# A two-layer streaming encoder on one core: the ConvFFN down projection as seven block products instead of a plain product

## The chip, the core and the metric

One core of a Trainium2 chip runs the whole program, and the metric is the time of one execution on the device in microseconds. Of three timed executions of the kernel before the median is 1671.96 us (1671.85 to 1672.4). The engines are named as in the profile: PE multiplies matrices, PEld loads its stationary operand, DVE, ACT and POOL work on vectors (POOL also issues DMAs here after the change), and SP issues most DMAs.

## The reference

Two layers run over 512 prompt positions and 32 sample positions, with 1024 features. Each layer has a mixing block, cross-attention, and a convolutional feed-forward block of width 2816, the part that is changed:

```
g, up = jnp.split(h @ w_up, 2, axis=-1)
gp = jnp.concatenate([hist, g], axis=1)
c = conv_b + sum(conv_w[j] * gp[:, j:j + S] for j in range(CONV_W))
a = jax.nn.silu(c) * up
return a @ w_down, gp[:, -(CONV_W - 1):]
```

The result of `a @ w_down` is added to the residual `x`. Everything is float32.

## The kernel before

Activations lie feature-major: `x` is a tile of 128 partitions by 8 feature blocks by 544 positions (512 prompt and 32 sample), and a product's output for one feature block is two PSUM banks of 272 positions each (`NSPL`). Accuracy of float32 comes from splitting each operand into a high part that PE can take (fp32r) and the rest: ACT makes the high part, DVE subtracts it to get the low part, and PE multiplies high by high, high by low and low by high. So each block of 128 by 128 weights costs three matmuls per bank (`proj_fm`, L256 to L266).

Weights come through `emit_unit` (L124): SP loads a unit of up to 1024 float32 per partition into `raw` (three buffers), ACT casts it (L134), and DVE takes the rest (L135), both into one of four `hl` buffers. `pop` hands out two units and emits two more, so that the splitting runs one step ahead of PE. SP's next load of `raw` waits until DVE has finished with the buffer.

`do_ffn` (L898 to L962) works in two halves of 11 feature blocks each. For two blocks at a time PE makes the gate, DVE scales it and convolves, ACT takes a tanh, and then PE makes the up branch, DVE scales it and multiplies it in, and the product is split into an `at` tile (L174, L175). After a half's 11 blocks follows its share of the down projection: for each of 8 output blocks `ct`, 11 blocks of weights by three by two banks are 66 matmuls into `pfda` and `pfdb` (L958), and then two adds on DVE from PSUM into `x` (`update_x`, L210). After the second half `after(ct)` makes the next layer's operand (`set_h`: ACT L190, DVE L191, ACT L197, POOL L202), or, in the last layer, transposes `x` on PE and stores it (`final_x`, L964).

The framework simulates the program when it is built and sets the order of instructions on every engine from that; on the chip each engine then runs its own list in order. Semaphores make it wait for other engines and for DMAs.

Of the kernel before, what the change touches and what calls it, by code (L numbers as in the profile page):

```python
# [18 lines left out]
SP = 512  # L19
# [4 lines left out]
HF = NF // 2  # L24
# [10 lines left out]
def encoder_step(ctx: ExitStack, tc: tile.TileContext, a, o):  # L35
# [46 lines left out]
    units = []  # L82

    def build_units():
        for l in range(DEPTH):
            wi = a["w_in"][l]
            def ks(src, k0, n):
                return src[k0 * 128:(k0 + n) * 128].rearrange("(k p) c -> p k c", p=128)

            def two(tag, mat, cols):  # L90
                for k0 in (0, 4):
                    units.append((tag, [ks(mat[:, c:c + n], k0, 4) for c, n in cols], 4, sum(n for _, n in cols)))

# [6 lines left out]
            for j in range(4):  # L100
                src = a["w_out"][l][:, 256 * j:256 * j + 256].rearrange("(b q k p) c -> q b p k c", b=2, q=2, p=128)
                for q in range(2):
                    units.append((f"wout{j}", [src[q, 0], src[q, 1]], 4, 256))
# [6 lines left out]
            for hf in range(2):  # L110
                for f in range(hf * HF, hf * HF + HF, 2):
                    w = 128 * min(2, hf * HF + HF - f)
                    for nm, c0 in (("g", 0), ("up", FF)):
                        two(f"{nm}{f}", a["w_up"][l], [(c0 + 128 * f, w)])
                for ct in range(8):
                    for k0, n in ((0, 8), (8, HF - 8)):
                        units.append((f"dn{hf}_{ct}", [ks(a["w_down"][l][:, 128 * ct:128 * ct + 128],
                                                          hf * HF + k0, n)], n, 128))
# [3 lines left out]
    state = {"emitted": 0, "popped": 0}  # L122

    def emit_unit(i):  # L124
        tag, srcs, n, wc = units[i]
        raw = wp.tile([128, 1024], F32, tag="raw", bufs=3, name="raw")
        rv = raw[:, 0:n * wc].rearrange("p (k c) -> p k c", k=n)
        k0 = c0 = 0
        for v in srcs:
            kn, cn = v.shape[1], v.shape[2]  # L130
            sp.dma_start(out=rv[:, k0:k0 + kn, c0:c0 + cn], in_=v)
            k0, c0 = (k0, c0 + cn) if kn == n else (k0 + kn, c0)
        hl = wp.tile([128, 2, 1024], F32R, tag="hl", bufs=4, name="hl")
        act.copy(hl[:, 0, 0:n * wc], raw[:, 0:n * wc])  # L134
# [998 lines left out]
```

## Time and profile before

| | us |
|---|---|
| median of 3 | 1671.96 |
| the profiled execution | 1672.13 |
| its span, first to last instruction | 1670.4 |
| PE busy | 1647.6 |
| DVE busy | 1006.9 |
| ACT busy | 725.4 |
| POOL busy | 267.1 |

The profile comes from one execution. What it doesn't cover of that execution's time is 1672.13 - 1670.4 = 1.73 us. A row of a timeline has a start, a duration, an engine, a line of the code, the operation and its tiles, and in brackets the idle time before it with what ended it. Matmuls are pipelined, so that the distance between two starts, not a row's duration, is what one costs.

### The profile page before, as it was taken

To read this page: it belongs to the slowest core of one execution; us is meant where nothing else is said; L and a number is where in the kernel's file an instruction comes from. 1 tells how busy PE (TensorE), PEld (TensorE's weight loads), DVE (VectorE), ACT (ScalarE), POOL (GpSimd) and SP (SyncE) were. 2 spreads that over 40 slices of the span, in tenths; PEclk is the share of its full clock that TensorE was granted. 3 is DMA by queue.
4 is the path that set the end of the run, shared out by engine and by line. 5 is a ranking of instruction groups with operands and counts; after the bars stand their busy time and mean duration, and the time that the engine had idled before them with its cause. 6 is when DMAs were issued, how large, how long until landed. Compare 5 with 4: busy or idle time off the path is not lost.

```text
span 1670.4 us, 32582 instructions
## 1 busy us (share of the span) xinstructions
PE 1647.6 (99%) x13115; PEld 1619.0 (97%) x13115; DVE 1006.9 (60%) x2219; ACT 725.4 (43%) x1481; POOL 267.1 (16%) x718
## 2 busy tenths in 40 slices
PE   7999999999999999999999999999999999999998
PEld 6999999999999999999999999999999999999998
DVE  6779755655476625665358786655555664366642
ACT  5467654544333312333345685545443332233321
POOL 4110033222111000100121000432311110011100
PEclk9999999999999999999999999999999999999999
DMA  6323234332222233313332322244322222332231
GB/s 178 93 88 100 71 102 128 125 110 89 89 90 70 84 88 102 101 58 90 96 120 72 94 71 77 90 132 133 115 82 88 79 77 88 103 92 86 67 111 56
DMA packets 200989, 158.04 MB, mean 95 GB/s; under 512 B 8670, under 2 KB 200038, under 8 KB 200838
## 3 DMA queue, kind: packets, MB, share of 16 engines
q1 hardware_dynamic: 200774, 155.82, 30.6%
q8 instruction: 103, 1.69, 0.4%
q14 instruction: 48, 0.39, 0.1%
q10 hardware_dynamic: 64, 0.14, 0.0%
HBM read 144.83 MB, written 11.10 MB: 93 GB/s over the span
## 4 chain that ended last, share of the span: by engine, by line
PE 94%; DVE 2%; ACT 2%; issue 1%; POOL 1%; DMA 0%; ACTq 0%
PE pfda L262 8%; PE pfua L262 8%; PE pfga L262 8%; PE pfdb L262 8%; PE pfub L262 8%; PE pfgb L262 8%; PE pr L279 3%; PE pr L281 3%; PE pr L280 3%; PE pwob L262 3%; PE pwoa L262 3%; PE pwca L262 3%; PE pqb L262 3%; PE pqa L262 3%; PE pwcb L262 3%; PE pm L281 2%
## 5 line engine op out<-in xcount | busy, mean ns | idle before, releaser
L135 DVE TENSOR_TENSOR hl<-raw,hl 128x1024 fp32r<-128x1024 f32 (+2 forms) x280 | 315.3, 1127 | 253.9 <-ACT hl L134 253.5
L134 ACT CAST hl<-raw 128x1024 fp32r<-128x1024 f32 (+2 forms) x280 | 270.1, 965 | 399.2 <-PE pfdb L262 137.3
L262 PE MATMUL pfda<-at,hl 128*128 128x272 f32 x1056 | 266.6, 289 | 0.0
L262 PE MATMUL pfdb<-at,hl 128*128 128x272 f32 x1056 | 266.3, 288 | 0.0
L262 PE MATMUL pfga<-hx,hl 128*128 128x272 f32 x1056 | 263.8, 287 | 0.0
L262 PE MATMUL pfgb<-hx,hl 128*128 128x272 f32 x1056 | 263.7, 287 | 0.0
L262 PE MATMUL pfua<-hx,hl 128*128 128x272 f32 x1056 | 259.3, 287 | 0.8 <-ACT rbc L252 0.8
L262 PE MATMUL pfub<-hx,hl 128*128 128x272 f32 x1056 | 259.1, 287 | 0.0
L262 PEld LDWEIGHTS pfda<-at,hl 128*128 128x128 f32 x1056 | 199.2, 189 | 0.0
L262 PEld LDWEIGHTS pfdb<-at,hl 128*128 128x128 f32 x1056 | 198.7, 188 | 0.1
L262 PEld LDWEIGHTS pfga<-hx,hl 128*128 128x128 f32 x1056 | 198.6, 188 | 0.0
L262 PEld LDWEIGHTS pfgb<-hx,hl 128*128 128x128 f32 x1056 | 198.4, 188 | 0.0
L262 PEld LDWEIGHTS pfua<-hx,hl 128*128 128x128 f32 x1056 | 196.3, 188 | 1.1 <-ACT rbc L252 1.1
L262 PEld LDWEIGHTS pfub<-hx,hl 128*128 128x128 f32 x1056 | 196.2, 188 | 0.0
L280 PE MATMUL pr<-hl,hx 128*128 128x256 f32 x512 | 146.2, 286 | 1.8 <-DVE hl L135 1.8
L281 PE MATMUL pr<-hl,hx 128*128 128x256 f32 x512 | 146.4, 287 | 1.4 <-DVE hx L191 1.4
L279 PE MATMUL pr<-hl,hx 128*128 128x256 f32 x512 | 145.1, 284 | 2.2 <-DVE vs L305 0.9
L279 PEld LDWEIGHTS pr<-hl,hx 128*128 128x128 f32 x512 | 97.9, 192 | 3.8 <-DVE vs L305 1.4
L280 PEld LDWEIGHTS pr<-hl,hx 128*128 128x128 f32 x512 | 97.1, 190 | 2.3 <-DVE hl L135 2.0
L281 PEld LDWEIGHTS pr<-hl,hx 128*128 128x128 f32 x512 | 96.9, 190 | 2.2 <-DVE hx L191 1.8
L262 PE MATMUL pwcb<-co,hl 128*128 128x272 f32 x384 | 87.0, 288 | 0.0
L262 PE MATMUL pwca<-co,hl 128*128 128x272 f32 x384 | 87.0, 289 | 0.0
(365 smaller groups left out, 3345.1 us busy)
## 6 DMA issues: line engine op xcount, KB each, us to landing
raw<-in_w_up_dram SPq DMA_DIRECT2D x80, 512.0 KB
raw<-in_w_down_dram SPq DMA_DIRECT2D x32, 512.0 KB
raw<-in_w_in_dram SPq DMA_DIRECT2D x24, 512.0 KB
raw<-in_w_in_dram SPq DMA_DIRECT2D x32, 256.0 KB
raw<-in_w_out_dram SPq DMA_DIRECT2D x32, 256.0 KB
raw<-in_wq_c_dram SPq DMA_DIRECT2D x16, 512.0 KB
raw<-in_wk_c_dram SPq DMA_DIRECT2D x16, 512.0 KB
raw<-in_wv_c_dram SPq DMA_DIRECT2D x16, 512.0 KB
```

Of the source, the lines that this page charges most:

```text
L134: act.copy(hl[:, 0, 0:n * wc], raw[:, 0:n * wc])
L135: vec.tensor_tensor(out=hl[:, 1, 0:n * wc], in0=raw[:, 0:n * wc], in1=f32(hl[:, 0, 0:n * wc]), op=ALU.subtract)
L262: pe.matmul(out=ps[0 if n0 == 0 else 1][:, 0:nn], lhsT=hl[:, wpart, kk, col * 128:col * 128 + 128], rhs=mv[:, n0:n0 + nn], start=first and ...
L279: pe.matmul(out=out, lhsT=lh(k), rhs=hl[:, 0, k % 4], start=(k == 0), stop=False)
L280: pe.matmul(out=out, lhsT=lh(k), rhs=hl[:, 1, k % 4], start=False, stop=False)
L281: pe.matmul(out=out, lhsT=ll(k), rhs=hl[:, 0, k % 4], start=False, stop=(k == k8 - 1))
```

## The change

The contraction blocks are taken in pairs, the output blocks `ct` in pairs, and the two banks of positions are the other pair, so that the down projection is a product of 2 by 2 blocks, and seven block products (Strassen's, in Winograd's form) take the place of eight. The weights' sums S1 to S4 are made by POOL from two `raw` tiles, the activations' sums T1 to T4 by POOL from the unsplit `up` tiles; all are split into high and low parts as before.

The 11 pairs of blocks go in three parts of 3, 4 and 4 pairs. A part has four groups `j` (two output blocks each) of seven products, with n = 3 or 4 pairs contracted by each, so 3n matmuls of 272 columns. Each group has three banks. Bank `p7a` is summed in four steps: after A11·B11, after S2·T2 and after S3·T3 the running sum is copied out by ACT (`snap`) and added to a quarter of `x` by a DMA that accumulates, issued by POOL; after A22·T4 DVE adds it to `x`. The partial sums in the other two banks are added by DVE as well: `p7c` after S1·T1 and after S4·B22, and `p7b` after A12·B21. The seventh product of a group (A22) stands after the second product of the next group. The first pair of the next part is computed before a part's down projection.

`hl` now has eight half-sized buffers: a down product takes one, other units two. `raw` has three as before; a group needs two of them at once. The tanh's factor 0.5 goes into the convolution's weights, and POOL multiplies the gate by the row scale that DVE multiplied into the up branch.

```
-HF = NF // 2
+PARTS = ((0, 3), (3, 7), (7, 11))
...
+    raws, items = [], []
+    LAST = "A22"
+    ORDER = ("A11", "S1", "S2", "S4", "A12", "S3")
...
+                n = p1 - p0
+                before = None
+                for j in range(4):
+                    src = a["w_down"][l][256 * p0:256 * p1, 256 * j:256 * j + 256].rearrange(
+                        "(k e p) c -> e p k c", e=2, p=128)
+                    for e in range(2):
+                        raws.append([[(0, n, 0, 256, src[e])], n, None])
+                    ids = (len(raws) - 2, len(raws) - 1)
+                    for m, it in enumerate(ORDER):
+                        item(f"dn{q}_{j}", it, ids, n)
+                        if m == 1 and before is not None:
+                            item(f"dn{q}_{j - 1}", LAST, before, n)
+                    before = ids
+                item(f"dn{q}_3", LAST, before, n)
...
+    SLOTS, RAWS = 8, 3
...
+            (A11, A21), (A12, A22) = [[raw_t[r][:, :, 128 * c:128 * c + 128] for c in range(2)] for r in ids]
+            def summed(name, in0, in1, op):
+                t = tmp([128, 4, 128], name, tag="c2", bufs=3)[:, 0:n]
+                pool.tensor_tensor(out=t, in0=in0, in1=in1, op=op)
+                sums[name] = t
+            if what == "A11":
+                summed("S1", A21, A22, ALU.add)
+                summed("S2", sums["S1"], A11, ALU.subtract)
+            src = {"A11": A11, "A12": A12, "A22": A22}.get(what)
+            if src is None:
+                src = sums[what]
+            hl = wp.tile([128, 2, 4, 128], F32R, tag="hl", bufs=SLOTS, name="hl")[:, :, 0:n]
+            act.copy(hl[:, 0], src)
+            vec.tensor_tensor(out=hl[:, 1], in0=src, in1=f32(hl[:, 0]), op=ALU.subtract)
+            wt[i] = hl
+            if what == "S1":
+                summed("S3", A11, A21, ALU.subtract)
+                summed("S4", A12, sums["S2"], ALU.subtract)
+        state["emitted"] += 1
+        load()
...
+    def cost(i):
+        return 2 if items[i][1] is None else 1
+    def prefetch(slots=SLOTS):
+        while state["emitted"] < len(items) and state["held"] + cost(state["emitted"]) <= slots:
+            state["held"] += cost(state["emitted"])
+            emit_item()
...
+            act.activation(out=th, in_=ct, func=AF.Tanh)
+            vec.scalar_tensor_tensor(out=ct, in0=th, scalar=1.0, in1=ct, op0=ALU.add, op1=ALU.mult)
+            pool.tensor_tensor(out=ct, in0=ct, in1=rbc, op=ALU.mult)
+            cc.append(ct)
+        wu = pop(f"up{i}")
+        us = []
+        for j in range(2):
+            ps = psR2("pfu", cnt)
+            cnt += 1
+            proj_fm(ps, j, x_parts(wu))
+            up = tmp([128, T], "up")
+            for v, n0, nn in halves(ps):
+                vec.tensor_tensor(out=up[:, n0:n0 + nn], in0=v, in1=cc[j][:, n0:n0 + nn], op=ALU.mult)
+            us.append(up)
+        h0, h1 = slice(0, TH), slice(TH, T)
+        (sB, sT, sU, sD), d = slots
+        ts = G("t4", [128, 4, TH], "ts")
+        pool.tensor_tensor(out=ts[:, 0], in0=us[0][:, h1], in1=us[0][:, h0], op=ALU.subtract)
+        pool.tensor_tensor(out=ts[:, 1], in0=us[1][:, h1], in1=ts[:, 0], op=ALU.subtract)
+        pool.tensor_tensor(out=ts[:, 2], in0=us[1][:, h1], in1=us[0][:, h1], op=ALU.subtract)
+        pool.tensor_tensor(out=ts[:, 3], in0=us[1][:, h0], in1=ts[:, 1], op=ALU.subtract)
+        dv = sD[:, :, d * TH:d * TH + TH]
+        split(dv[:, 0], dv[:, 1], us[0][:, h0])
+        split(sB[:, 0], sB[:, 1], us[1])
+        for k, t in enumerate((sT, sU)):
+            split(t[:, 0], t[:, 1], ts[:, 2 * k:2 * k + 2].rearrange("p j t -> p (j t)"))
+        bl = {"B11": dv, "B21": sB[:, :, h0], "B22": sB[:, :, h1], "T1": sT[:, :, h0], "T2": sT[:, :, h1],
+              "T3": sU[:, :, h0], "T4": sU[:, :, h1]}
+        return bl, cnt
...
+    SIX = (("A11", "B11", 0, True, (0, 0)), ("S1", "T1", 2, True, (1, 1)), ("S2", "T2", 0, False, (0, 1)),
+           ("S4", "B22", 2, False, (0, 1)), ("A12", "B21", 1, True, (0, 0)), ("S3", "T3", 0, False, (1, 1)))
+    def down(q, prs, done):
+        n = len(prs)
+        def product(tag, prod, banks, ct):
+            lf, rt, bk, new, (r, h) = prod
+            w, = pop(tag, 1)
+            ps = banks[bk][:, 0:TH]
+            for k in range(n):
+                m = prs[k][rt]
+                for wpart, part in ((0, 0), (0, 1), (1, 0)):
+                    pe.matmul(out=ps, lhsT=w[:, wpart, k], rhs=m[:, part],
+                              start=new and k == 0 and wpart + part == 0, stop=k == n - 1 and wpart == 1,
+                              skip_group_check=True)
+            xv = x[:, ct + r, h * TH:h * TH + TH]
+            if bk == 0 and lf != "A22":
+                cp_ = tmp([128, TH], "snap")
+                act.copy(cp_, ps)
+                pool.dma_start(out=xv, in_=cp_, accum_op=ALU.add)
+            else:
+                vec.tensor_tensor(out=xv, in0=ps, in1=xv, op=ALU.add)
+        def last(j, banks):
+            product(f"dn{q}_{j}", ("A22", "T4", 0, False, (1, 0)), banks, 2 * j)
+            done(2 * j)
+            done(2 * j + 1)
+        before = None
+        for j in range(4):
+            banks = [psR("p7a"), psR("p7b"), psS("p7c")]
+            for m, prod in enumerate(SIX):
+                product(f"dn{q}_{j}", prod, banks, 2 * j)
+                if m == 1 and j:
+                    last(j - 1, before)
+            before = banks
+        last(3, before)
...
-            for ct in range(8):
-                w2 = pop(f"dn{hf}_{ct}")
-                ps = psR2("pfd", cnt)
-                cnt += 1
-                proj_fm(ps, 0, [(w2[0], [(k, av[k][:, 0], av[k][:, 1]) for k in range(8)], True, False),
-                                (w2[1], [(k, av[8 + k][:, 0], av[8 + k][:, 1]) for k in range(HF - 8)], False, True)])
-                update_x(ct, ps)
-                if hf == 1:
-                    after(ct)
...
+        pairs[0], cnt = ffn_pair(l, 0, rbc, fc, cnt, slots(0))
+        for q, (p0, p1) in enumerate(PARTS):
+            for i in range(p0 + 1, min(p1 + 1, NF // 2)):
+                pairs[i], cnt = ffn_pair(l, i, rbc, fc, cnt, slots(i))
...
+            prs = [pairs.pop(i) for i in range(p0, p1)]
+            down(q, prs, after if p1 == NF // 2 else lambda ct: None)
```

Before the change PE runs the 66 matmuls of one `ct` after those of the other; after it, the products of two neighbouring groups alternate. The two places below are in the first part of the first layer. First POOL after the change, from the first accumulating DMA on (before, POOL has nothing in the down projection): `snap` is a copied sum, `x` the residual, S1 to S4 are sums of weights, and the waits on `DMAHW` are for loads of `raw`.

```order
L1063 DMA x_78<-snap_7116 128x272 [waits Activation_49]
L187 TENSOR_TENSOR S1_7195<-raw_7122,raw_7124 128x384 [waits DMAHW0_49,DMAHW7_49,DVE_49,Pool_49]
L1063 DMA x_78<-snap_7148 128x272 [waits Activation_49]
L187 TENSOR_TENSOR S2_7197<-S1_7195,raw_7122 128x384 [waits DVE_49,Pool_49]
L187 TENSOR_TENSOR S3_7217<-raw_7122 128x384 [waits DVE_49]
L187 TENSOR_TENSOR S4_7219<-raw_7124,S2_7197 128x384 [waits DVE_49,Pool_49]
```

The second accumulating DMA (the sum after S2·T2 of group 0) stands behind the first weight sum of group 2, which waits for two loads.

Next DVE at the same place, before the change: `hl` is a split weight unit, `x` the residual.

```order
L135 TENSOR_TENSOR hl_7448<-raw_7446,hl_7448 128x1024 [waits DMAHW7_49,Activation_49]
L210 TENSOR_TENSOR x_78<-pfda_7376,x_78 128x272 [waits PE_49]
L210 TENSOR_TENSOR x_78<-pfdb_7377,x_78 128x272 [waits PE_49]
L135 TENSOR_TENSOR hl_7453<-raw_7451,hl_7453 128x384 [waits DMAHW0_49,Activation_49]
L135 TENSOR_TENSOR hl_7528<-raw_7526,hl_7528 128x1024 [waits DMAHW1_49,Activation_49]
```

And DVE after the change; `DMASW` are the accumulating DMAs.

```order
L198 TENSOR_TENSOR hl_7199<-raw_7122,hl_7199 128x384 [waits DMAHW7_49,Activation_49]
L1065 TENSOR_TENSOR x_78<-p7c_7194,x_78 128x272 [waits PE_49]
L198 TENSOR_TENSOR hl_7214<-S1_7195,hl_7214 128x384 [waits Activation_49]
L1065 TENSOR_TENSOR x_78<-p7c_7086,x_78 128x272 [waits DMASW1_49]
L198 TENSOR_TENSOR hl_7231<-raw_6957,hl_7231 128x384 [waits PE_49,Activation_49]
L198 TENSOR_TENSOR hl_7248<-S2_7197,hl_7248 128x384 [waits Activation_49]
L198 TENSOR_TENSOR hl_7263<-S4_7219,hl_7263 128x384 [waits Activation_49]
L1065 TENSOR_TENSOR x_78<-p7a_7084,x_78 128x272 [waits PE_49]
```

An add that waited only for PE before now waits for an accumulating DMA in the fourth row, and the next splits stand behind it; the first of these (`raw_6957`, A22 of group 1) is the last reader of its `raw` buffer. On PE, 189 of the first part's 252 matmuls stand before the first that needs A12 of the last group, which on DVE is the third split behind A22 of group 2 (after S2 and S4 of group 3); in the parts of 4 pairs it is 264 or 252 of 336.

## Rows read from the trace of the kernel before

**Rows 1.** Page, part 1: busy us (share of the span) xinstructions.
```profile
span 1670.4 us, 32582 instructions
PE 1647.6 (99%) x13115; PEld 1619.0 (97%) x13115; DVE 1006.9 (60%) x2219; ACT 725.4 (43%) x1481; POOL 267.1 (16%) x718
```

**Rows 2.** PE's waits: us in total, times, longest.
```profile
PE pxina L997 <- DMA xin<-in_x_prompt_dram: 4.8, 1, 4.8
PE pr L280 <- DVE hl L135: 1.8, 1, 1.8
...
PE pyT L968 <- DVE x L210: 0.4, 1, 0.4
```

**Rows 3.** Page, part 4: the chain that ended last, by engine.
```profile
PE 94%; DVE 2%; ACT 2%; issue 1%; POOL 1%; DMA 0%; ACTq 0%
```

**Rows 4.** Groups by line and shape: xcount | busy us, mean ns | idle before.
```profile
L262 PE MATMUL pfda<-at,hl 128*128 128x272 f32 x1056 | 266.6, 289 | 0.0
L262 PE MATMUL pfdb<-at,hl 128*128 128x272 f32 x1056 | 266.3, 288 | 0.0
...
L202 POOL TENSOR_TENSOR ssq<-ssq,sqx 128x544 f32<-128x544 f32 x42 | 68.1, 1621 | 116.2 <-ACT sqx L197 115.8
...
L943 DVE SCALAR_TENSOR_TENSOR up<-up,ct 128x544 f32<-128x544 f32 x44 | 31.8, 723 | 1.1
...
L135 DVE TENSOR_TENSOR hl<-raw,hl 128x384 fp32r<-128x384 f32 x32 | 17.5, 548 | 0.0
...
L210 DVE TENSOR_TENSOR x<-pfda,x 128x272 f32<-128x272 f32 x32 | 13.9, 433 | 9.4 <-PE pfda L262 9.4
...
L135 DVE TENSOR_TENSOR hl<-raw,hl 128x512 fp32r<-128x512 f32 x16 | 11.1, 692 | 3.9 <-ACT hl L134 3.9
...
L134 ACT CAST hl<-raw 128x512 fp32r<-128x512 f32 x16 | 10.0, 622 | 25.5 <-PE pfub L262 13.0 <-PE pfgb L262 12.5
```

**Rows 5.** PE's timeline, two banks in turn: first and last of 72 starts.
```profile
1575.33 0.29 PE L262 MATMUL pfua<-hx,hl 128*128 128x272 f32 x1
...
1584.16 0.29 PE L262 MATMUL pfgb<-hx,hl 128*128 128x272 f32 x1
```

**Rows 6.** PE's timeline, one bank: first and last of 75 starts.
```profile
1095.20 0.28 PE L279 MATMUL pm<-hl,memT 128*128 128x256 f32 x1
...
1104.08 0.28 PE L281 MATMUL pm<-hl,memT 128*128 128x256 f32 x1
```

**Rows 7.** Timeline, a load of 512 KB: the buffer's last reader, the issues.
```profile
1311.46 1.22 DVE L135 TENSOR_TENSOR hl<-raw,hl 128x1024 fp32r<-128x1024 f32 x1 [1.06 <-ACT hl L134]
...
1312.71 3.60 SPq L131 DMA_DIRECT2D raw<-in_w_up_dram  x2
```

**Rows 8.** Stretches: busy by engine, PEclk, DMA share, GB/s (last).
```profile
1300.00:1430.00 130.00, 130.00 (x1045) 130.00 (x1044) 75.22 (x126) 40.22 (x52) 11.82 (x48) 1.00 0.28 83
...
1314.50:1315.50 1.00, 1.00 (x10) 1.00 (x9) 1.00 (x2) 0.65 (x1) 0.00 (x0) 1.00 1.04 361
1315.50:1316.50 1.00, 1.00 (x10) 1.00 (x9) 1.00 (x2) 0.00 (x0) 0.00 (x0) 1.00 0.19 64
```

**Rows 9.** Timeline, the last store of 256 KB: its issue.
```profile
1667.05 0.38 SPq L975 DMA_DIRECT2D out_yp_dram<-y  x1
```

**Rows 10.** Timelines of POOL and DVE, at the same times.
```profile
746.97 0.18 POOL L918 COPY gs<-gb 128x2 f32<-128x2 f32 x1 [12.40 <-DVE gb L913]
...
752.94 0.66 POOL L918 COPY gs<-gb 128x2 f32<-128x2 f32 x1 [2.84 <-DVE gb L913]
...
795.07 1.36 POOL L202 TENSOR_TENSOR ssq<-ssq,sqx 128x544 f32<-128x544 f32 x1 [7.67 <-ACT sqx L197]
...
752.87 0.69 DVE L135 TENSOR_TENSOR hl<-raw,hl 128x512 fp32r<-128x512 f32 x1
```

**Rows 11.** Timelines of ACT, DVE: the last block's operand for layer 1.
```profile
842.87 0.43 DVE L210 TENSOR_TENSOR x<-pfdb,x 128x272 f32<-128x272 f32 x1
...
844.78 0.92 DVE L191 SCALAR_TENSOR_TENSOR hx<-x,cols,hx 128x544 fp32r<-128x544 f32 x1
...
843.51 0.74 ACT L190 ACTIVATE hx<-x,cols 128x544 fp32r<-128x544 f32 x1
```

More of the change, by code (lines that the diff above doesn't have):

```diff
@@ L102, in build_units @@
                 for q in range(2):
-                    units.append((f"wout{j}", [src[q, 0], src[q, 1]], 4, 256))
+                    raws.append([[(2 * b, 2, 0, 256, src[q, b]) for b in range(2)], 4, None])
+                    item(f"wout{j}", None, (len(raws) - 1,), 4)
             for h in range(4):
@@ L120, in encoder_step @@
+        for i, (_, what, ids, _) in enumerate(items):
+            if what == "S1":
+                raws[ids[0]][2] = i
     gcol = {}
     wt = {}
[L122 to L134, printed above, removed]
-        vec.tensor_tensor(out=hl[:, 1, 0:n * wc], in0=raw[:, 0:n * wc], in1=f32(hl[:, 0, 0:n * wc]), op=ALU.subtract)
-        hl = hl[:, :, 0:n * wc].rearrange("p j (k c) -> p j k c", k=n)
-        wt[i] = hl
@@ L139, in prefetch, with load @@
-    def prefetch(upto):
-        while state["emitted"] < min(upto, len(units)):
-            emit_unit(state["emitted"])
-            state["emitted"] += 1
+    raw_t, sums = {}, {}
+    state = {"emitted": 0, "popped": 0, "held": 0, "loaded": 0}
+    SLOTS, RAWS = 8, 3
+    def load():
+        while state["loaded"] < len(raws):
+            r = state["loaded"]
+            if r >= RAWS and raws[r - RAWS][2] >= state["emitted"]:
+                return
+            loads, nk, _ = raws[r]
+            raw = wp.tile([128, 1024], F32, tag="raw", bufs=RAWS, name="raw")
+            rv = raw[:, 0:nk * 256].rearrange("p (k c) -> p k c", c=256)
+            for k0, kn, c0, cn, src in loads:
+                sp.dma_start(out=rv[:, k0:k0 + kn, c0:c0 + cn], in_=src)
+            raw_t[r] = rv
+            state["loaded"] += 1
@@ new lines, in emit_item @@
+    def emit_item():
+        i = state["emitted"]
+        tag, what, ids, n = items[i]
+        load()
+        if what is None:
+            hi, lo = [wp.tile([128, 1024], F32R, tag="hl", bufs=SLOTS, name="hl") for _ in range(2)]
+            src = raw_t[ids[0]].rearrange("p k c -> p (k c)")
+            act.copy(hi, src)
+            vec.tensor_tensor(out=lo, in0=src, in1=f32(hi), op=ALU.subtract)
+            wt[i] = tuple(v.rearrange("p (k c) -> p k c", c=256) for v in (hi, lo))
+        else:
[14 more added lines that the diff above has]
+            wt[i] = hl
+            if what == "S1":
+                summed("S3", A11, A21, ALU.subtract)
+                summed("S4", A12, sums["S2"], ALU.subtract)
+        state["emitted"] += 1
+        load()
@@ L295, in proj_tm @@
             for part in range(2):
[L296 removed]
+                pe.matmul(out=ps[0:64, 0:256], lhsT=xsm[:, k], rhs=w2[k // 4][part][:, k % 4],
                           start=(k == 0 and part == 0), stop=(k == 7 and part == 1))
@@ new lines, in do_ffn, with slots @@
+        pairs, held = {}, {}
+        def slots(i):
+            q = next(j for j, (p0, p1) in enumerate(PARTS) if p0 <= i < p1)
+            tags = held.setdefault(q, list(ATAGS[q]))
+            new = lambda: G(tags.pop(0), [128, 2, T], "at", F32R)
+            res = [new(), new(), new()]
+            d = (i - PARTS[q][0]) % 2
+            if d == 0:
+                held["d"] = new()
+            return res + [held["d"]], d
+        pairs[0], cnt = ffn_pair(l, 0, rbc, fc, cnt, slots(0))
+        for q, (p0, p1) in enumerate(PARTS):
+            for i in range(p0 + 1, min(p1 + 1, NF // 2)):
+                pairs[i], cnt = ffn_pair(l, i, rbc, fc, cnt, slots(i))
+            if p1 == NF // 2:
```

144 lines of the change are left out of this document (69 added, 75 removed).

## The prediction

> **What bounds the kernel now.** I read the page's busy times first: PE is busy for 1647.6 of 1670.4 us, so some 23 us at most are idle on the engine that everything else feeds [rows 1]. PE's waits say what these are: the largest is 4.8 us for the first input, and no other single line reaches 2 us in all [rows 2]. The chain that ended last is PE for 94% [rows 3]. So a matmul that goes is time that goes, and a wait that PE gets is time that comes, one for one. The down projection is 1056 matmuls into one bank and 1056 into the other [rows 4]. Their busy times overlap, so their price is the distance of starts: 72 starts of 272 columns, in two banks by turns, lie 8.83 us apart, 8.83 / 71 = 124.4 ns [rows 5].
>
> **What is removed.** Seven products for eight: 2112 x 7/8 = 1848, and 264 x 124.4 ns = 32.8 us less on PE. One thing may take a part back: the matmuls of a product now go one after another into one bank. A chain into one bank in this trace has 256 columns and 8.88 / 74 = 120.0 ns [rows 6]. At 2.4 GHz 256 columns are 106.7 ns and 272 are 113.3, so the single bank adds 13.3 ns and the two by turns 11.1. From nothing to 1848 x 2.2 ns = 4.1 us; I take 2.0.
>
> **What is added beside PE.** In the gate and up stage, a pair of blocks is 192 matmuls, 23.9 us. POOL gets two multiplications of 544 and four subtractions of 272, at 1.36 us for 544 when it runs alone [rows 10] some 5.5 us; DVE loses two multiplications of 0.72 us and gains 1.1 us of splits (816 elements more, at 0.692 us for 512) [rows 4]; ACT gains about as much. DVE is busy 75.22 of 130 us there, ACT 40.22 and POOL 11.82 [rows 8], so PE covers all of it, and would pay only if an up result came later than the next pair's banks are needed.
>
> In the down projection a group of n = 4 has 84 matmuls, 10.45 us, and one of n = 3 has 63, 7.84 us; a product is 1.49 or 1.12 us. DVE makes seven splits, at 0.692 us (512 wide) or 0.548 (384), and four adds of 0.433 [rows 4]: 6.6 and 5.6 us. ACT makes seven casts at 0.622 us [rows 4] and three copies below that: at most 6.2 us. POOL makes four sums, at 1.36 x 512/544 = 1.28 us each or 0.96, and issues three DMAs: no row has a DMA of POOL's; SP holds 0.38 us for one [rows 9], and a POOL sum, 1.36 us, bounds it from above, so 6.3 to 9.2 us and 5.0 to 7.9. Each engine fits into the group's time, with POOL nearest to it, and the sums of the first two groups of a part are made while PE still does the gate and up stage.
>
> **The new waits.** What doesn't fit by shares may still be late by its order. There is one ring of waits per group: DVE's split of A22 frees a `raw` buffer; SP loads both halves of the group after next; POOL's S1 waits for both loads; the accumulating DMA of S2·T2 is queued behind S1 on POOL; DVE's add of S4·B22 waits until that DMA has landed, because it adds to the same quarter of `x`; and the next group's split of A22 is queued behind this add. Its pieces:
> - the split, 0.69 us;
> - the loads. One freed at 1312.68 us (1311.46 + 1.22) was issued at 1312.71 [rows 7], moved at 361 GB/s for a microsecond and ended in the stretch up to 1316.5, which had only 64 GB/s left [rows 8]: 3.5 us. The second 512 KB add 1.5 us at that rate: 5.0 us (n = 3: 4.2);
> - S1 and a little queueing, 1.7 us (1.35);
> - the DMA from issue to landing. None of its kind is in the trace. The last store, 256 KB, is issued at 1667.05 and the span ends at 1670.4 [rows 9]: 3.35 us. This one has 139 KB but also reads what it adds to. From 2 us (the load's 3.5 without its 1.5 of data) to 7 us (twice the store); I take 3.0, nearest to the store;
> - the add, 0.43 us.
>
> Together C = 10.8 us for n = 4 and 9.5 for n = 3. That is more than a group's PE time, so it is the head start that matters. The first split of A22 ends after two products, an add and itself: 4.1 us into the part (3.2); two rounds and three more splits later (2.1, 1.65) A12 of the last group is ready. That is at 4.1 + 21.6 + 2.1 = 27.8 us, and PE wants it after 252 or 264 matmuls, 31.3 or 32.8 us: hidden, with 3.5 us to spare. For n = 3 it is 3.2 + 19.0 + 1.65 = 23.9 against 189 matmuls, 23.5 us: 0.4 us late. I count 1 us for each of the two parts of n = 3, 2.0.
>
> The page "DMA: Bandwidth & Descriptors" of the Trainium skill (section "Anatomy of one DMA — SWDGE (gpsimd) path") gives a POOL-issued DMA 2.0 us and its bytes at 436 GB/s, an estimate of 2.3 us here. By that both rings would be hidden, and the sum 2 us lower; the store's row is a microsecond above it, and I stay with the row.
>
> **The last parts.** There the group's end brings more work. In layer 0, two POOL sums of 1.36 us per group [rows 10] and DVE's operand at 0.8 us stand in the same ring; in layer 1, PE's transposes for the output wait for quarters of `x` that only a landed DMA completes. With two sums in it, C is 13.5 and the last group's A12 is ready at 33.2 us against 31.3. I count 2 us each, 4.0.
>
> **The two ends.** Before, the last adds (0.43 us) are followed by ACT 0.74 and DVE 0.92 [rows 11], and PE works on meanwhile. After, the last quarter of `x` comes by copy (0.6) and DMA (3.0) and then goes the same way (1.6), 5.2 us after S3·T3, while PE has A22 (1.5) and about 1.3 us of the next layer's matmuls that don't need it: 2.4 us of wait. At the very end A22 waits 0.6 us for the copy of its bank, and the DMA lands about 1.7 us after the last matmul where before two adds took 0.9: 1.4, say 2.0 with the transposes of two blocks instead of one.
>
> **The sum.** 1672.1 (the profiled execution, 0.2 above the median) - 32.8 + 2.0 (bank) + 2.0 + 4.0 (waits in the parts) + 2.4 + 2.0 (ends) = 1651.7; forecast 1652 us.
>
> **Rivals.**
> *All hidden.* If the DMA lands within 2 us and one bank costs no more than two, only the two ends are left, at about 3 us: 1672.1 - 32.8 + 3 = 1642. For it: PE's waits of before are tiny although ACT and DVE are idle half the time just before a split. Against: nothing of before has a DMA between two vector instructions.
>
> *The ring sets the pace, and it is slower.* Its place is DVE's add behind the accumulating DMA. The losses in the six parts are 2(2C - 18.7) for the two of n = 3 and 2(2C - 25.1) + 2(2C - 26.6) for the others; with C of n = 3 shorter by 1.3 this is 12C - 146 in all. The other losses without the 4.0 and 2.0 are 6.4, so the gain is used up at 12C - 146 = 26.4, C = 14.4, a landing after 6.6 us instead of 3.0. At 8 us C is 15.8: 1672.1 - 32.8 + 6.4 + 43.6 = 1689. For it: POOL queues each DMA behind sums that wait for loads, and loads and accumulations share the DMA engines. Against: these are busy for 28% of the time [rows 8].
>
> *POOL and DVE hold each other up.* A 0.18 us POOL copy took 0.66 us when it met a DVE split that began 0.07 us before it, and ended with that split [rows 10]; and L202 takes 1621 ns on average [rows 4] against 1.36 alone. If the sums and splits of a group never overlap, they need 5.1 + 4.8 = 9.9 us of 10.45, and with the DMAs' issues (1.1) and the adds (1.7) 12.7; the head start of two groups' sums (10.2 us a part) pays for that where n = 4 (50.8 - 10.2 = 40.6 of 41.8), but a part of n = 3 has 42.2 - 7.7 = 34.5 against 31.4, and layer 0's last part has 10.9 of POOL sums and 6.3 of DVE more. Some 6 + 14 us on the forecast: 1670 or a little more, about no change. The page "SBUF — State Buffer" of the Trainium skill ("SBUF: two separate sides") states such an exclusive lock, between a DVE instruction with two SBUF inputs and a POOL one that reads SBUF; the copy's row agrees.
>
> **Chances and range.** The forecast (1646 to 1662) 0.45; all hidden (1639 to 1646) 0.18; the ring 0.23; the mutual hold-up 0.14. What a measurement of this kernel can tell from no change is 0.2%, 3.3 us. Faster than 1668.6 are the first two, a third of the third rival and a little of the ring with a landing near 6 us: 0.69. Within it: 0.07. Slower: 0.24. The range 1640 to 1684 leaves out the fastest corner and landings above 7.5 us (C = 15.3, 1683).
>
> **What would show it.** In the profile after: 1848 matmuls at 124 to 127 ns; PE's waits for DVE's splits (`hl`) in the groups 2 and 3 of a part, hardly any in groups 0 and 1, and more in the part of 3 pairs; DVE's longest waits at the add for an accumulating DMA, about 3 us after its issue; 2 to 3 us of PE's wait at the next layer's first projection. A landing above 6 us, or a wait of PE for ACT's copy of a bank in every group, would make the forecast wrong; so would POOL sums of over 2 us.

## The result and the profile after

The changed kernel takes 1708.51 us (median of 4 runs, 1706.72 to 1714.13) against 1671.9 before: a ratio of 1.0225, 95% interval 1.0201 to 1.0249. The forecast was 1652. The profiled execution spans 1705.0 us.

The page's busy times of after, to be read against [rows 1]:

```profile
PE 1640.1 (96%) x12851; PEld 1601.5 (94%) x12851; DVE 1187.9 (70%) x2347; ACT 809.5 (47%) x1693; POOL 643.7 (38%) x1020
```

The 264 matmuls are gone, but PE is busy only 7.5 us less, not 32.8, and it is idle for 65 us instead of 23. Its four largest waits, where [rows 2] had no other line of 2 us than the first input (columns: us in total, times, longest):

```profile
PE p7c L1055 <- DVE x L1065: 9.6, 7, 3.5
PE p7a L1055 <- DVE hl L198: 8.8, 6, 2.7
PE pxina L1144 <- POOL ql L513: 4.6, 1, 4.6
PE p7c L1055 <- DVE at L249: 4.4, 2, 2.2
```

The third is the first input again. The new ones are for DVE: its adds into x, the splits of weights (hl), and the splits of the T blocks (at). The chain that ended last was PE for 94% [rows 3]; now all else holds 30% of it:

```profile
PE 70%; DVE 12%; POOL 6%; DMA 5%; issue 4%; ACT 2%; SPq 0%; POOLq 0%; DVEq 0%; ACTq 0%
```

What DVE, ACT and POOL wait for in turn closes a ring: DVE for the accumulating DMA, ACT's casts for POOL's sums, POOL's issue of the DMA for ACT's copy.

```profile
POOL x L1063 <- ACT snap L1062: 59.9, 20, 7.7
DVE x L1065 <- DMA x<-snap: 56.3, 27, 4.9
ACT hl L197 <- POOL S L187: 56.2, 33, 4.6
```

The groups by line and shape (xcount | busy us, mean ns of one | idle before). A split of 512 columns took 692 ns before [rows 4] and takes 1020 to 1209 now; the split of `up`, 544 columns, 722 ns before (the last row, from the trace of before), takes 1250. A sum of POOL's takes 1464 to 1547 ns where the prediction had 1280, and one of its subtractions for the T blocks (ts), 272 columns, 1042 to 1545 ns where it had 680.

```profile
L198 DVE TENSOR_TENSOR hl<-S,hl 128x512 fp32r<-128x512 f32 x64 | 64.8, 1020 | 4.8 <-ACT hl L197 4.7
L198 DVE TENSOR_TENSOR hl<-raw,hl 128x512 fp32r<-128x512 f32 x48 | 58.0, 1209 | 0.7 <-ACT hl L197 0.7
L249 DVE TENSOR_TENSOR at<-up,at 128x544 fp32r<-128x544 f32 x22 | 27.5, 1250 | 1.4 <-ACT at L248 1.4
L187 POOL TENSOR_TENSOR S<-raw,S 128x512 f32<-128x512 f32 x16 | 24.8, 1547 | 3.8 <-DVE hl L198 3.8
L187 POOL TENSOR_TENSOR S<-raw 128x512 f32<-128x512 f32 x32 | 46.9, 1464 | 36.2 <-DMA raw<-in_w_down_dram 21.3 <-DVE x L1065 8.7 <-DVE hl L198 6.2
L1026 POOL TENSOR_TENSOR ts<-up 128x272 f32<-128x272 f32 x22 | 22.9, 1042 | 0.9 <-DVE up L1021 0.9
L1027 POOL TENSOR_TENSOR ts<-up,ts 128x272 f32<-128x272 f32 x22 | 34.0, 1545 | 54.4 <-DVE up L1021 54.4
L1028 POOL TENSOR_TENSOR ts<-up 128x272 f32<-128x272 f32 x22 | 27.2, 1237 | 0.0
L1029 POOL TENSOR_TENSOR ts<-up,ts 128x272 f32<-128x272 f32 x22 | 27.5, 1252 | 0.0
L1063 POOL DMA_DIRECT2D x<-snap x72 | 65.0, 993 | 64.8 <-ACT snap L1062 59.9 <-ACT hl L197 4.9
L175 DVE TENSOR_TENSOR at<-up,at 128x544 fp32r<-128x544 f32 x44 | 31.8, 722 | 20.0 <-ACT at L174 20.0
```

One turn of the ring, in layer 0's last part. ACT has copied a bank at 828.73 (first fence, ACT's timeline). The DMA that adds it to x is issued by POOL only at 836.67 (second fence, POOL's): it stands behind a sum that waited 4.33 us for a load, a sum of squares and two more sums. So 7.9 us go by in POOL's queue. This is the longest of the 72 turns: from the end of the copy to the issue of its DMA the median is 2.2 us, and 22 of them take under 0.5. The DMA lands in 4.82 us and ends DVE's wait of 4.24 us (third fence, DVE's); PE, which needs the bank that the add reads, has stood for 3.48 us when the add ends (fourth fence, PE's).

```profile
828.37 0.36 ACT L1062 COPY snap<-p7a 128x272 f32<-128x272 f32 x1
```

```profile
830.12 1.84 POOL L187 TENSOR_TENSOR S<-raw 128x512 f32<-128x512 f32 x1 [4.33 <-DMA raw<-in_w_down_dram]
831.92 1.37 POOL L276 TENSOR_TENSOR ssq<-ssq,sqx 128x544 f32<-128x544 f32 x1
833.25 1.75 POOL L187 TENSOR_TENSOR S<-S,raw 128x512 f32<-128x512 f32 x1
834.96 1.76 POOL L187 TENSOR_TENSOR S<-raw 128x512 f32<-128x512 f32 x1
836.67 0.83 POOL L1063 DMA_DIRECT2D x<-snap  x1
```

```profile
841.51 0.44 DVE L1065 TENSOR_TENSOR x<-p7c,x 128x272 f32<-128x272 f32 x1 [4.24 <-DMA x<-snap]
```

```profile
842.01 3.09 PE L1055 MATMUL p7c<-at,hl 128*128 128x272 f32 x12 [3.48 <-DVE x L1065]
844.89 2.92 PE L1055 MATMUL p7b<-at,hl 128*128 128x272 f32 x12
847.61 1.80 PE L1055 MATMUL p7a<-at,hl 128*128 128x272 f32 x12
```

And the stall is not the whole price. The next 24 matmuls start over 847.61 - 842.01 = 5.60 us, 233 ns each instead of 124.4 [rows 5]. The stretches show why (PE busy stands first, the granted clock, PEclk, third from the end): PE does nothing for 3.5 us, and then runs at half clock, 1.2 GHz, until about 848.

```profile
838.50:842.00 3.50, 0.03 (x1) 0.00 (x0) 0.49 (x2) 1.15 (x3) 2.05 (x3) 0.87 1.12 253
842.00:843.00 1.00, 0.99 (x4) 0.99 (x5) 1.00 (x2) 1.00 (x2) 0.00 (x0) 0.50 0.72 114
844.00:845.00 1.00, 1.00 (x6) 1.00 (x6) 1.00 (x1) 1.00 (x3) 0.71 (x1) 0.50 0.00 0
848.00:849.00 1.00, 1.00 (x11) 1.00 (x9) 1.00 (x4) 0.00 (x0) 0.00 (x0) 1.00 0.85 128
```

The 3.5 us of waiting cost 3.5 + 5.60 - 24 x 0.1244 = 6.1 us.

Most waits are not of this kind. PE stands for over 1 us nine times between its down products, 20.7 us in all. Six of the nine, 14.1 us, come about 50 to 83 matmuls into a part, one in each part; two more come after 146 of 252, and the turn above after 240 of 336. In the first part DVE's split of 384 columns, 548 ns before [rows 4], takes 2.86 us while POOL makes two sums, and PE waits 2.66 us for it:

```profile
557.68 2.86 DVE L198 TENSOR_TENSOR hl<-raw,hl 128x384 fp32r<-128x384 f32 x1
557.88 1.29 POOL L187 TENSOR_TENSOR S<-S,raw 128x384 f32<-128x384 f32 x1
558.84 1.27 POOL L187 TENSOR_TENSOR S<-raw 128x384 f32<-128x384 f32 x1
560.59 1.49 PE L1055 MATMUL p7a<-at,hl 128*128 128x272 f32 x7 [2.66 <-DVE hl L198]
```

In the second part the first add of a bank stands behind splits of 1.2 to 1.3 us, beside which POOL makes the T blocks of the pair computed ahead:

```profile
688.10 1.30 DVE L249 TENSOR_TENSOR at<-up,at 128x544 fp32r<-128x544 f32 x1
689.33 1.24 DVE L198 TENSOR_TENSOR hl<-raw,hl 128x512 fp32r<-128x512 f32 x1
690.49 0.43 DVE L1065 TENSOR_TENSOR x<-p7c,x 128x272 f32<-128x272 f32 x1
688.78 1.24 POOL L1029 TENSOR_TENSOR ts<-up,ts 128x272 f32<-128x272 f32 x1
690.97 3.09 PE L1055 MATMUL p7c<-at,hl 128*128 128x272 f32 x12 [2.18 <-DVE x L1065]
```

By stage, from PE's timelines (mixing: from PE's first matmul, or from the end of FFN 0, up to the first gate product of the layer; FFN: from there to the end of the last down product; us; the kernels are those of the next section):

| kernel | mixing 0 | FFN 0 | mixing 1 | FFN 1 |
|---|---|---|---|---|
| before | 439.0 | 398.6 | 420.0 | 402.5 |
| after | 443.9 | 417.6 | 422.6 | 410.1 |
| plain down projection, rest of the change | 444.5 | 398.4 | 423.4 | 402.2 |
| the same with the old buffers | 438.8 | 398.6 | 420.1 | 402.5 |
| adds on DVE | 443.9 | 402.1 | 420.7 | 395.5 |
| adds on DVE, no weight sums | 444.4 | 386.2 | 422.2 | 385.5 |
| the fastest that computes the whole result | 438.9 | 393.4 | 419.4 | 387.1 |

The FFN stages should have become 16.4 us shorter each and are 19.0 and 7.6 longer; the mixing stages, where nothing is computed differently, are 7.5 longer.

### The profile page after: what moved, and what is told of

It reads as the page before. It is cut to its first block, busy times and chain, and to the rows that moved or that the text cites. A ratio compares the mean times of both kernels' runs of the same rounds, so it can differ in the third digit from the quotient of the medians.

```text
span 1705.0 us, 32990 instructions
## 1 busy us (share of the span) xinstructions
PE 1640.1 (96%) x12851; PEld 1601.5 (94%) x12851; DVE 1187.9 (70%) x2347; ACT 809.5 (47%) x1693; POOL 643.7 (38%) x1020
## 4 chain that ended last, share of the span: by engine, by line
PE 70%; DVE 12%; POOL 6%; DMA 5%; issue 4%; ACT 2%; SPq 0%; POOLq 0%; DVEq 0%; ACTq 0%
PE pfua L336 6%; PE pfga L336 6%; PE pfub L336 6%; PE pfgb L336 5%; DVE hl L198 5%; DMA x<-snap 3%; PE pr L353 3%; PE pr L355 3%; PE pr L354 3%; PE pwoa L336 3%; PE pwca L336 3%; PE pqb L336 3%; PE pwob L336 3%; POOL S L187 3%; PE pqa L336 3%
## 5 line engine op out<-in xcount | busy, mean ns | idle before, releaser
L180 DVE TENSOR_TENSOR hl<-raw,hl 128x1024 fp32r<-128x1024 f32 x208 | 263.1, 1266 | 102.6 <-ACT hl L179 97.1
L179 ACT CAST hl<-raw 128x1024 fp32r<-128x1024 f32 x208 | 218.6, 1051 | 196.3 <-PE pfub L336 53.3
L336 PE MATMUL pfgb<-hx,hl 128*128 128x272 f32 x1056 | 254.0, 287 | 0.2 <-DVE x L1065 0.2
L336 PE MATMUL pfga<-hx,hl 128*128 128x272 f32 x1056 | 254.1, 288 | 0.0
L1055 PE MATMUL p7a<-at,hl 128*128 128x272 f32 x1056 | 154.2, 296 | 10.1 <-DVE hl L198 8.8
L1055 PEld LDWEIGHTS p7a<-at,hl 128*128 128x128 f32 x1056 | 142.7, 195 | 14.0 <-DVE hl L198 10.1
L276 POOL TENSOR_TENSOR ssq<-ssq,sqx 128x544 f32<-128x544 f32 x42 | 68.6, 1632 | 81.9 <-ACT sqx L271 81.4
L1055 PE MATMUL p7c<-at,hl 128*128 128x272 f32 x528 | 84.5, 308 | 14.1 <-DVE x L1065 9.6
L1055 PEld LDWEIGHTS p7c<-at,hl 128*128 128x128 f32 x528 | 76.7, 206 | 16.1 <-DVE x L1065 11.2
L197 ACT CAST hl<-S 128x512 fp32r<-128x512 f32 (+1 forms) x96 | 56.0, 583 | 72.3 <-POOL S L187 56.2
```

What stands on the lines that cost most here:

```text
L179: act.copy(hi, src)
L180: vec.tensor_tensor(out=lo, in0=src, in1=f32(hi), op=ALU.subtract)
L197: act.copy(hl[:, 0], src)
L276: pool.tensor_tensor(out=ssq_t["x"], in0=ssq_t["x"], in1=sq, op=ALU.add)
L336: pe.matmul(out=ps[0 if n0 == 0 else 1][:, 0:nn], lhsT=hl[wpart][:, kk, col * 128:col * 128 + 128], rhs=mv[:, n0:n0 + nn], start=first and ...
L1055: pe.matmul(out=ps, lhsT=w[:, wpart, k], rhs=m[:, part], start=new and k == 0 and wpart + part == 0, stop=k == n - 1 and wpart == 1, skip_ ...
```

## The experiments

Times are medians; before is 1671.4 to 1672.1 in all of them, after 1708.5. All edits are to the kernel after. In the down projection every group has seven splits on DVE, four sums S1 to S4 on POOL, three quarter sums by copy and DMA, four by DVE. The texts of what was expected call PE TensorE, DVE VectorE, ACT ScalarE, POOL GpSimd and SP SyncE.

**Is it the block products at all?** The down projection made plain again:

```
-  for m, prod in enumerate(SIX): product(...)      # seven block products
+  for col in range(2): proj_fm(ps, col, ...); update_x(2 * j + col, ps)
```

> The kernel after with the plain down projection of before (eight block products, no sums of blocks, two banks, x added to by VectorE), but with all else of the change: the slots, ct x rbc on GpSimd, the parts of 3, 4 and 4 pairs. If the loss sits in the down projection itself (its ring of waits, its sums, its part starts), this is before plus the 5.9 us that the first layer's mixing stage lost: 1672 to 1680 us. If what was done around the products (smaller tiles, multiplications moved to GpSimd) costs as well, it is above 1685.

1680.5 us (1.0050, 1.0027 to 1.0073). FFN stages as before to 0.3 us, mixing stages 8.9 slower. So 8.6 us of the loss have nothing to do with the products, and the goal for the products was 1680.5 - 32.8 = 1647.7.

**The DMAs, the sums, and both.**

```
-            if bk == 0 and lf != "A22":      # copy and accumulating DMA
+            if False:                        # all adds on DVE
```

> The kernel after, but all 168 quarter sums are added into x by VectorE straight from PSUM; no copy by ScalarE, no DMA that accumulates. Theory 1 (the DMA's landing, median 3.7 us, inside the ring of waits, and its queueing behind GpSimd's sums, sets the pace): over 20 us faster than after, below 1688. Theory 2 (GpSimd's sums and VectorE's splits hold each other up, and the DMA only fills time that is lost anyway): within 8 us of after, since VectorE gets 72 adds of about 0.43 us more. Theory 3 (the last pair's sums for the T blocks at each part's start, and the clock that falls after such a wait): within 10 us of after.

1674.5 us (1.0018, 1.0007 to 1.0030): 34.0 faster than after. Then the copies stay and the DMAs are left out, so that three of seven products never reach x:

```
-                pool.dma_start(out=xv, in_=cp_, accum_op=ALU.add)
```

> The kernel after with ScalarE's copies but without the 72 DMAs that accumulate, so three of seven products of each group never reach x. Theory 1: over 20 us faster than after, as with VectorE's adds, and some microseconds more because VectorE has no more to do. Theory 2: 5 to 10 us faster (72 issues of 0.99 us leave GpSimd). Theory 3: under 10 us faster.

1674.7 us (1.0013, 1.0001 to 1.0024): the same, so 72 more adds on DVE cost nothing that shows. Next the weight sums are left out and raw blocks take their places:

```
-                pool.tensor_tensor(out=t, in0=in0, in1=in1, op=op)
-                sums[name] = t
+                sums[name] = A21 if name == "S1" else A12 if name == "S4" else A22
```

> The kernel after without GpSimd's 96 sums of weight blocks (the four products that need one take a raw block instead). Theory 1: 10 to 20 us faster, since a ring loses one sum of 1.5 us and the DMA's queueing behind the others, but keeps loads and landing. Theory 2: over 20 us faster than after, with VectorE's splits of 512 back at about 0.7 us instead of 1.0 to 1.2. Theory 3: under 10 us faster.

1662.6 us (0.9946, 0.9921 to 0.9971): 45.9 faster than after, with the DMAs still there. More than theory 1 allowed.

Both edits together:

> All adds by VectorE and no sums of weight blocks (four products of seven take a raw block instead): both suspects away at once. Taken alone, the accumulating DMAs were worth 34 us and the sums 46. If the two are separate prices, this is 1708.5 - 80 = 1629, below what 33 us of matmuls can explain; if they are two parts of one ring of waits, so that either alone breaks most of it, it ends near the floor of 1680.5 (the plain down projection) - 33 = 1647 us, 1647 to 1657.

1649.7 us (0.9866, 0.9837 to 0.9894), 58.8 faster, not 34.0 + 45.9 = 79.9: much of the loss goes with either of the two. Without both the products give most of what was counted: the FFN stages are 12.2 and 16.7 shorter than the plain ones, 28.9 of 32.8. The subtractions for the T blocks are still on POOL there, and the split of `up` beside them is still slow (second row). PE's busy time for the same 12851 matmuls is in the first row:

```profile
PE 1616.1 (98%) x12851; PEld 1586.4 (96%) x12851; DVE 1134.7 (69%) x2419; ACT 791.0 (48%) x1621; POOL 456.8 (28%) x852
L247 DVE TENSOR_TENSOR at<-up,at 128x544 fp32r<-128x544 f32 x22 | 25.5, 1157 | 1.4 <-ACT at L246 1.4
```

It is 24.0 us less than after's 1640.1; the other 32.7 of the 56.7 us between the two spans (1705.0 and 1648.3) are idle time. Of the 24.0, the clock explains at most 14.8: the mean granted clock is 0.9889 in after and 0.9975 here, and 0.0111 x 1705.0 - 0.0025 x 1648.3 is 14.8. The rest was not taken apart; every interruption of a stream of matmuls also shows the last one's full length as busy, 0.29 us where starts lie 0.124 apart.

**What of the DMA costs: its landing, or its place on POOL?** The DMA writes beside its own source, so that nobody who reads x waits for it; and, as a control, the same two copies without a DMA:

```
+                cp_ = tmp([128, 2, TH], "snap")
+                act.copy(cp_[:, 0], ps); act.copy(cp_[:, 1], ps)
+                pool.dma_start(out=cp_[:, 1], in_=cp_[:, 0], accum_op=ALU.add)   # control: left out
```

> The kernel after with its 72 accumulating DMAs going into the second half of their own buffer (filled by a second copy of ScalarE's), so that nothing that reads x waits for them; three of seven products don't reach x. GpSimd's issue time, the queue behind its sums and the traffic stay; only the wait for the landing goes. If that wait is the price: like the run without the DMAs, 1670 to 1680. If it is GpSimd's time and queue: 1698 to 1708.

> The control for the run whose DMAs went into their own buffer: the same two copies by ScalarE, but no DMA (three of seven products don't reach x). If what that run kept of the loss (1697.8) is GpSimd's issue and the queue behind it: 1672 to 1680, as without the DMAs. If it was ScalarE's second copy: 1690 or more.

1697.8 us (1.0154, 1.0124 to 1.0183) and 1674.1 us (1.0015, 1.0004 to 1.0026). The wait for the landing is worth 10.7 us, the DMA itself on POOL 23.7: its issue, and the sums that stand behind it while it waits for ACT's copy, and so for PE. Its traffic is in the 23.7 too and was not tried alone; but POOL's sums wait no longer for their loads with it than without it, 28.0 us in after and 35.7 with all adds on DVE.

**Sums on DVE.**

```
-                pool.tensor_tensor(out=t, in0=in0, in1=in1, op=op)
+                vec.tensor_tensor(out=t, in0=in0, in1=in1, op=op)
```

> The kernel after, accumulating DMAs kept, with the four weight sums of a group on VectorE instead of GpSimd. VectorE then has 7 splits, 4 sums and 4 adds per group, 9.3 us of 10.45 at the durations of before; GpSimd has only its DMAs to issue. If GpSimd's sums matter because they slow VectorE and make the DMA queue behind them: near the run without the sums (1662.6), below 1680. If only VectorE's own load or the landing of the DMA matters: no faster than after, 1700 or more.

1682.7 us (1.0071, 1.0038 to 1.0103): 25.8 faster than after, a little short of what was expected. Two things change at once: DVE's splits have no sums beside them, and the DMAs have no sums before them on POOL. DVE has 96 sums more, 66.6 us by their rows, and is busy 1167.9 us, 20.0 less than in after, mostly because its splits come down from 1020 and 1209 ns:

```profile
L198 DVE TENSOR_TENSOR hl<-S,hl 128x512 fp32r<-128x512 f32 x64 | 47.2, 743 | 1.5 <-ACT hl L197 1.4
L198 DVE TENSOR_TENSOR hl<-raw,hl 128x512 fp32r<-128x512 f32 x48 | 38.2, 796 | 0.8 <-ACT hl L197 0.8
```

**The loads in the ring.** A22 is split right behind its own group's S3, which frees its raw buffer earlier; first alone, then with all adds on DVE:

```
-  ..., S3, (next group:) A11, S1, A22, S2, ...
+  ..., S3, A22, (next group:) A11, S1, S2, ...     # order of the splits; products as they were
```

> The kernel after with A22 split directly behind its own group's S3, not behind S1 of the next group, so that its raw buffer comes free, and the load after it starts, two splits earlier; the products keep their order. If the ring over the raw buffers and the loads (as the prediction drew it) sets the pace: over 15 us faster than after, below 1693. If GpSimd's queue sets it (sums that stand behind DMAs that wait for ScalarE's copy of a bank): within 8 us of after.

> All adds on VectorE, and A22 split early as in the run before. Without the DMAs on GpSimd the loads are the only thing that ties the sums to TensorE's progress. If so: 1655 to 1665. If the sums' own length beside VectorE's splits is the rest: 1670 to 1676, no change from 1674.5.

1697.3 us (1.0154, 1.0125 to 1.0184), 11.2 faster than after, between the two expectations; and 1674.4 us (1.0016, 1.0004 to 1.0027), no change. The loads are a part of the ring while the DMAs hold POOL, and none without them.

**What is left without the DMAs.** Two of four sums to DVE (S3 and S4):

```
+                (vec if name in ("S3", "S4") else pool).tensor_tensor(out=t, in0=in0, in1=in1, op=op)
```

> All adds on VectorE, S1 and S2 on GpSimd, S3 and S4 on VectorE: VectorE has 7 splits, 7 adds and 2 sums, 9.2 us of 10.45 at the durations of before, and GpSimd's share of the ring is halved. If the sums on GpSimd and their slowing of VectorE are the rest of the loss: 1655 to 1666. If VectorE's load decides: 1675 or more.

1668.6 us (0.9982, 0.9971 to 0.9993), 5.9 better; then POOL's four subtractions for the T blocks left out:

```
-        ts = G("t4", [128, 4, TH], "ts")     # and its four subtractions
-            split(t[:, 0], t[:, 1], ts[:, 2 * k:2 * k + 2]...)
+            split(t[:, 0], t[:, 1], us[k])
```

> All adds, S3 and S4 on VectorE (1668.6), without GpSimd's four subtractions per pair for the T blocks (their products take the plain blocks, so the output is another). If the last pair's T blocks, which TensorE waits for at each part's start, and the clock that falls there still cost: 8 us or more faster, below 1661. If they cost little: within 4 us.

1650.5 us (0.9873, 0.9853 to 0.9893): 18.1 us for something that the prediction had at zero. That is the price of POOL's time, of the slower splits and of the later T blocks together, and it holds beside S1 and S2 on POOL: the kernel of 1649.7 us keeps these subtractions, has no weight sums, and its products lose 3.9 us in all. The split of a 544-wide block is back at its time of before (here all 66 of them, in one group):

```profile
L249 DVE TENSOR_TENSOR at<-up,at 128x544 fp32r<-128x544 f32 x66 | 44.9, 717 | 1.4 <-ACT at L248 1.4
```

**The 8.6 us of the mixing stages.** The loads of all other weights issued one by one again (with all adds on DVE), then, in the plain kernel, also the old buffer for both halves of a split:

```
-        load()                                             # up to three buffers ahead
+        load(max(ids) + 1 if what is None else None)       # what this split needs
-            hi, lo = [wp.tile([128, 1024], F32R, tag="hl", bufs=SLOTS, name="hl") for _ in range(2)]
+            hl2 = wp.tile([128, 2, 1024], F32R, tag="hl", bufs=SLOTS // 2, name="hl")
```

> The kernel with all adds on VectorE (1674.5), and the weight loads outside the down projection issued again one by one with the split that uses them, as before the change, not three ahead. If the 8.6 us that the mixing stages lost (1680.5 against 1671.9 with a plain down projection) come from the order of SyncE's loads: 1665 to 1669. If they come from anything else (other pools, other order on TensorE): 1672 to 1677.

> The plain down projection once more (1680.5 us with the change's slots), now with the two halves of a split weight in one buffer and the loads issued one by one, as before the change. The planner then puts the whole first mixing stage in the order of before on every engine. If the 8.6 us come from the order that the planner found: 1670 to 1674. If from something else of the change (parts of 3, 4 and 4 pairs, multiplications on GpSimd): above 1677.

1674.2 us (1.0013, 1.0001 to 1.0024), no change from 1674.5: the loads alone don't explain it. 1671.9 us (1.0001, 0.9990 to 1.0011) with both: the whole of the 8.6 is back. The planner then lists the first mixing stage on PE, DVE, ACT and SP row for row as before. So the cause lies in the new buffers, alone or with the loads, and the order that the planner finds with them; order and buffers went back together, so that the order by itself does it is likely, but not shown. Why that order is slower was not followed further.

**Versions that use this.** All adds, S3 and S4 on DVE, old buffers (two block products share one):

```
+                state["half"] = wp.tile([128, 2, 2, 4, 128], F32R, tag="hl", bufs=SLOTS // 2, name="hl")
```

> All adds on VectorE, S3 and S4 on VectorE, S1 and S2 on GpSimd (1668.6 us so far), with the old buffers: one for both halves, two block products of the down projection sharing one, loads one by one. If the order found by the planner is worth 8 us by itself: 1658 to 1663. If sharing a buffer costs the down projection its look-ahead: 1668 or more.

1659.1 us (0.9921, 0.9904 to 0.9937): faster than before. With S1 and S2 on DVE in place of S3 and S4:

> As the run before, but S1 and S2 on VectorE, S3 and S4 on GpSimd. S1 waits for the loads of two buffers, and on VectorE everything queued behind it would wait too, so if the queue behind a waiting sum matters, this is 3 us or more slower than the run before; if only the number of sums on each engine matters, the same within 2 us.

1670.1 us (0.9990, 0.9980 to 1.0001): 11.0 slower for the same number of sums. S1 waits for loads, 20.6 us in all on DVE, and the adds and splits behind it wait too; which engine's queue holds the waiting sum matters more than how many it has.

Last, the T blocks' subtractions on DVE, all four or the first two:

```
-        pool.tensor_tensor(out=ts[:, 0], in0=us[0][:, h1], in1=us[0][:, h0], op=ALU.subtract)
+        vec.tensor_tensor(out=ts[:, 0], in0=us[0][:, h1], in1=us[0][:, h0], op=ALU.subtract)
```

> The kernel with all adds, S3 and S4 on VectorE and the old buffers (1659.1), with the four subtractions for the T blocks on VectorE too: 4 x about 0.43 us per pair more for VectorE. If GpSimd's subtractions cost by slowing VectorE's splits beside them (the 544-wide split of `up` took 1126 ns with them and 720 without), VectorE gets the price back and the T blocks come sooner: 1645 to 1656. If VectorE's own load decides: 1660 or more.

> As the run before, but only T1 and T2 on VectorE, T3 and T4 on GpSimd. If the slowing is the price, about half of the other run's gain over 1659.1; if the chain of four subtractions on one engine is the price, as much as or more than the other run.

1650.3 us (0.9867, 0.9850 to 0.9883) and 1653.4 us (0.9891, 0.9876 to 0.9906). The first is the fastest kernel that computes the whole result, 21 us ahead of before and 58 ahead of after. Its DVE does 88 subtractions more than at 1659.1, four groups like the second row below with 18.9 + 9.6 + 9.6 + 9.5 = 47.6 us in all, and is busy 1195.6 us where it was 1203.1: the splits beside them got 45.3 us faster by their rows, about as much. Half of the subtractions gave 5.7 of the 8.9 us, nearer to half than to all.

```profile
PE 1621.5 (98%) x12851; PEld 1589.5 (96%) x12851; DVE 1195.6 (73%) x2555; ACT 782.5 (47%) x1621; POOL 416.7 (25%) x812
L1039 DVE TENSOR_TENSOR ts<-up,ts 128x272 f32<-128x272 f32 x22 | 9.6, 438 | 0.5
L261 DVE TENSOR_TENSOR at<-up,at 128x544 fp32r<-128x544 f32 x22 | 15.8, 716 | 0.0
```

## Why the prediction was wrong

- *Removed, 32.8 us: right. The single bank, 2.0: not there.* Without POOL's sums and DMAs the FFN stages gain 28.9 us, so part boundaries, ends and T blocks together take 3.9 there. In one bank the starts lie 125.0 ns apart in that kernel (median), and 126.0 in the two banks of before's down projection: one bank costs nothing.
- *The waits in the parts, 2.0 + 4.0 us: the term that failed.* Without it and the bank the sum is 1672.1 - 32.8 + 2.4 + 2.0 = 1643.7, with the 8.6 of the mixing stages 1652.3; measured are 1708.5, so some 56 us stand in place of 6.0, and 58.8 go when POOL's weight sums and DMAs go.
- *"Each engine fits into the group's time": the step that failed first.* By shares it still fits: POOL's four sums at 1.46 to 1.55 us and three issues at 0.99 are some 9 us of 10.45, inside the 6.3 to 9.2 of the prediction; DVE's seven splits are 7.7 us at 1.02 and 1.21 instead of 4.8 at 0.692, and with four adds 9.4. But the prices were taken where the engines don't meet, and a share doesn't say when an engine is free: a split stood 2.86 us beside two sums, a DMA 7.9 us behind others.
- *The gate and up stage at nothing: wrong for the same reason.* DVE, ACT and POOL each had room by their shares, but the four T subtractions, put at 4 x 0.68 = 2.7 us of POOL a pair, take 5.1 (111.6 us for 22 pairs), the split of `up` 1.25 us instead of 0.72, and leaving the subtractions out gave 18.1 us (1668.6 to 1650.5) beside S1 and S2 on POOL.
- *"It is the head start that matters": there was hardly any.* The prediction let PE wait at A12 of the last group, after 189 of 252 or 252 and more of 336 matmuls, and hardly in the groups 0 and 1. PE has no wait of 1 us there; six of its nine come in the first two groups, for splits and adds that were late beside POOL's sums and T subtractions.
- *The ring, C = 10.8: it exists, but too short.* Its pieces "S1 and a little queueing, 1.7" and "from issue to landing, 3.0" both failed. Landing has a median of 3.7 us (2.7 to 7.7), and the wait for it was worth 10.7 us in all. The queue ahead of the issue alone was 2.2 us at the median and 7.9 in the turn shown, and 23.7 of the DMAs' 34.4 us went with their place on POOL (1697.8 to 1674.1). The ring was drawn as if POOL took each piece when it was ready. It takes them in order, so a DMA stood behind a sum that waited for a load, and the next sums behind a DMA that waited for PE.
- *The rival "the ring sets the pace" gave the sign.* Its condition, a landing above 6.6 us, did not come at the median: 3.7 was enough. Its price was more in the queue than in the landing.
- *The rival "POOL and DVE hold each other up" had the mechanism but a price of no change.* Moving the weight sums gave 25.8 us, in part because the DMAs then have no sums before them; moving the T subtractions, with no DMAs, gave 8.9. How much of the whole loss is hold-up and how much is queue stays open. The page "SBUF — State Buffer" of the Trainium skill ("SBUF: two separate sides") states an exclusive lock, held for a whole instruction, between a DVE instruction with two SBUF inputs and a POOL one that reads SBUF. The rows agree: 1250 ns beside POOL's subtractions, 717 without; and DVE's adds that read PSUM take 432 to 439 ns in after, 433 before [rows 4].
- *The 2.3 us for a POOL-issued DMA*, an estimate from the page "DMA: Bandwidth & Descriptors" of the Trainium skill ("Anatomy of one DMA — SWDGE (gpsimd) path"), is below even the shortest landing here, 2.7 us. The measurement decides.
- *Not in the sum at all*: the clock after a stall (2.6 us on top of 3.5 in the turn shown, at most 14.8 in all against the kernel without sums and DMAs), and the stages that the change doesn't touch, which came in another order with the new buffers and loads, 8.6 us.
- *The ends, 2.4 and 2.0 us: near.* PE waits 2.6 us for x at layer 1's first projection; from the last product to the end of the span 6.2 us pass, 5.4 before.

## What to carry to other kernels

Shares of busy time don't say whether work fits beside the bound engine: list what stands in each engine's queue in order, and ask of every instruction that can wait what is queued behind it. Durations for added work are to be taken from rows where the engines meet, and here a subtraction or sum on POOL is to be charged to DVE's splits as well. Here a change to buffers and loads changed the planner's order in stages that it didn't touch, so compare the stages that should be the same before explaining the others.

## What was not expected of the hardware

- A wait of PE of about 3.5 us was followed by some 6 us at a granted clock of 0.50, at 233 ns per matmul instead of 124.4; the six other waits of 2 us and more in after's down projection were each followed by a shorter stretch at 0.50, and the mean clock of the span is 0.989 where before it was 0.998.
- POOL's issue of a DMA takes 0.99 us of its own (72 issues, 65.0 us), and the 136 KB that add to x land 3.7 us after it at the median.
- DVE got faster in total when it was given 47.6 us of POOL's work.
